# A list scheduler and its task clock charge a single-pass matmul a longer fixed time

## Chip, cores and metric

The kernel runs on one core of a Trainium2 chip. The metric is the device time of one execution in microseconds (us). A core has a tensor engine (PE, whose weight loads are shown as PEld), a vector engine (DVE), a scalar engine (ACT), GpSimd (POOL) and a sync engine (SP) that here issues DMAs only. Each executes its own instructions in the order in which the program gives them and waits for the others by semaphores.

## The reference, cut to what matters

Two layers over 512 tokens of width 1024, in float32. A layer mixes tokens by three branches, adds the input, normalizes, goes through a gated feed-forward and normalizes again:

```python
z = x @ w_in[l]                      # one projection, its columns shared out to the branches
y_a = a_b * causal_dwconv(a_c * a_v, conv_a_w)
y_b = diff_attention(dq, dk, dv, lam, lam_init, subln_g)
y_c = nsa_attention(nq, kc, ..., cmp_pos, phi_w1, phi_w2)   # compressed, selected and window keys
gates = sigmoid(m_g)
merged = sum(gates[:, :, i] * (y_i @ w_branch[i]))
x = layer_norm(ALPHA * x + merged @ w_o, ln1_g, ln1_b)
h = causal_dwconv(x @ w_up, conv_w) + conv_b
a, u = split(h)
x = layer_norm(ALPHA * x + (gelu(a) * u) @ w_down, ln2_g, ln2_b)
```

dq, dk, nq and three of the six key and value parts get rotary embeddings first.

## The kernel before, in words

Nearly all time is matrix products at float32 accuracy. Each operand is split into a high and a low part (xh and xl of the activations, wh and wl of the weights), and a product is three single-pass matmuls into one bank of PSUM, high by high, high by low and low by high (`mm3`). Weights come in 290 units of 128 x 1024 words: SP loads raw, ACT copies it to wh, DVE (or POOL, for a few units around a change of phase) subtracts to wl; raw, wh and wl have three buffers each. A projection (`g_proj`) is eight mm3 of 512 columns, 24 matmuls, into one of three banks of tag mm.

The order of the work is made in two steps, before the program is issued.

`Sched` runs tasks, which are generators that emit instructions. A task gives back a delay in ns, an event, or nothing, and the first ready task in order of priority goes on. What "ready" means is told by `sch.now`, a clock that `mm` and `tr` push on by what they think a matmul or a transpose takes on PE. The delays are the constants `DLY` (line 115): for instance `norm`, 4025 ns, from the instructions of a token tile's norm to its transposes. `g_fill` at priority 9 fills the waits with projections, gates and branches.

`Recorder.schedule` then takes all recorded instructions, with their costs by `Recorder.cost`, and lists them: on each engine, at each moment of its model, the first instruction in order of tracing whose inputs are there and whose buffers can be had goes next. `issue` emits the result in that order. So the costs decide the order on every engine; how long things take on the chip is another matter.

The pieces that the text below speaks of:

- `rope` (two operations of DVE from the bank, one of POOL, one sum on DVE) makes a query or key head ready. `g_cmp` then multiplies it with the compressed keys, four small matmuls sc<-kcc per head for four heads in a layer, after a delay `rope`.
- `g_tok_norm` makes the products with the tokens on partitions (w_o and w_dn). For each token tile of 128 the last three units are multiplied together, 3 units x 2 x 3 = 18 matmuls of 512 columns, then a task `g_norm` is started: statistics, mean, the power of the variance on POOL (`rsqrt`, out s<-s,mhalf), scaling and bias on DVE, and after `DLY["norm"]` two times four transposes (tp<-cst,tmp), each followed by a split into xh (ACT) and xl (DVE).
- `g_halves` is the next phase's beginning: three banks, first for tokens 0 to 255 and then for 256 to 511, in matmuls of 256 columns, as soon as the events of the norm allow. The weights wl of these units are made on POOL.

Of the kernel before, what the change touches and what calls it, by code (L numbers as in the profile page):

```python
# [26 lines left out]

# [1 line left out]
def _t_block(w, cols):  # L29
# [68 lines left out]
def _smalls(inp, l):  # L98
    """Per-layer constants that sit on partitions: [128, .]"""
    p = []  # L100
    p.append(inp["ffn_conv_w"][l].reshape(3, 44, 128).transpose(2, 1, 0).reshape(128, 132))
    p.append(inp["ffn_conv_b"][l].reshape(44, 128).T)
    p.append(inp["conv_a_w"][l].reshape(3, 4, 128).transpose(2, 1, 0).reshape(128, 12))
    p.append(inp["nsa_cmp_pos"][l].reshape(2, 16, 128).transpose(2, 0, 1).reshape(128, 32))
    p.append(inp["diff_subln"][l].reshape(128, 1))
    p.append(np.broadcast_to(inp["diff_lambda"][l].reshape(1, 256), (128, 256)))
    p.append(np.concatenate([inp["nsa_phi_w2"][l, i] for i in (0, 0, 1, 1)], axis=1))
    return np.concatenate(p, axis=1)
# [4 lines left out]
N_UNITS = 290  # L113
# time (ns) that the other engines take until the tensor engine can go on with what a step has made
DLY = dict(norm=4025, xsplit=2550, t2=11900, gelu=439.8, ctr=1000, rope=3680, stack=3150, cmp=40500, score=245, soft=1600, psplit=1700, pvfree=529.2, dsoft=875, dsoft_n=21, dat=200, dnorm=9000, dscore=1960)
# [4 lines left out]

# [1 line left out]
def _dims(side, sizes, known):  # L122
# [14 lines left out]
def _rearrange(idx, pattern, known):  # L137
    """einops on the free dimensions (the partition dimension p stays first)"""
    lhs, rhs = (_dims(x, None, None) for x in pattern.split("->"))
# [20 lines left out]
class RAP:  # L160
    """an access pattern of a recorded tile: where it lies, and how to get it from the real tile"""

# [44 lines left out]
class Recorder:  # L207
    # ns from the end of an instruction to the start of one that needs it
    LAT = {("PE", "PE"): 0, ("ACT", "ACT"): 0, ("DVE", "DVE"): 127, ("POOL", "POOL"): 97, ("ACT", "PE"): 230,
# [58 lines left out]
    def cost(eng, name, args, kw, op):  # L268
# [7 lines left out]
        if eng == "PE":  # L276
# [4 lines left out]
            if b.dtype == F32R:  # L281
                return nb / 2.4 + 3 if nb >= 256 else max(110, nb / 0.6)
            return 216 * max(1, nb / 128)
# [19 lines left out]
    def schedule(self):  # L303
        """list scheduling in order of tracing; slots of a tag are given in order of first use"""
        import heapq
# [26 lines left out]
        def slots(op):  # L332
            """None if the slots can be had now, else when (or inf)"""
            need = {}
# [103 lines left out]
class Sched:  # L438
    """Orders the tensor engine's work: tasks are generators that emit instructions and yield a delay in ns,
    an Event, or None; the first ready task in order of priority goes on.  now is the tensor engine's clock."""  # L440

# [31 lines left out]
def trunk(ctx, tc, xT_d, x_d, w_d, cst_d, sm_d, w1_d, gb_d, out_d, order):  # L473
# [46 lines left out]

# [1 line left out]
    def mm(o, a, b, start, stop):  # L522
        T.matmul(o, a, b, start=start, stop=stop)
        n = math.prod(b.shape[1:])
        if b.dtype == F32R:
            sch.now += n / 2.4 + 3 if n >= 256 else max(107, n / 0.6)
        else:
# [10 lines left out]

# [1 line left out]
    cst = cp.tile([128, NCST], F32, tag="cst", name="cst")  # L540
# [8 lines left out]

# [1 line left out]
    def unit(*key, parts=1, lo=None):  # L551
# [27 lines left out]
    def g_halves(x, evs, keys):  # L579
        """the first products of a phase, by token halves, as the norm before it delivers them"""  # L580
        us = []
# [26 lines left out]
    def stack_q(z, a0, a1):  # L608
        """a0 = [hi of rows 0:64; their lo], a1 = [lo of rows 64:128; their hi]"""
        lo = tmp(F32R)  # L610
# [6 lines left out]
    def stack_k(z, h0, h1, l0, l1):  # L617
        """h0 = [hi; hi] of rows 0:64, h1 of rows 64:128, l0, l1 the same of the lo parts"""
        for h, lo, r, o in ((h0, l0, LO, HI), (h1, l1, HI, LO)):
# [5 lines left out]
    def softmax(o, n, mx, sums):  # L625
        """exp((o + causal mask) / 8 - its row maximum), the row sums into sums; mx is left at minus the maximum"""
        e = tmp()
# [5 lines left out]
    def rsqrt(v, n, r=None, o=None):  # L633
        """(v + eps) ** -0.5"""
        if r is None:
# [8 lines left out]

# [1 line left out]
    def g_tok_norm(l, kind, nk, lhs, res_d, gi, last):  # L646
        """norm(ALPHA * x + lhs^T w): the next x (transposed and split, per token tile an event, and in DRAM)"""
        r, st = [], []
# [51 lines left out]
        for n in range(2):  # L700
            o = [bank(b) for b in (("mm", "mm", "mm", "sc") if n == 0 else ("sc", "pv", "mm", "mm"))]

            # the columns of a token tile's products; the very last ones in two halves, each in a bank
            cols = [[(o[t], 0, 512)] for t in range(4)]
# [39 lines left out]
    def g_layers():  # L744
# [1 line left out]
        X = new_x()  # L746
# [25 lines left out]
    def g_layer(l, X, evs, res_d):  # L772
        lam_init = 0.8 - 0.6 * math.exp(-0.3 * l)

# [1 line left out]
        smf = cp.tile([128, 176], F32, tag="smf", name=nm("smf"))  # L776
# [10 lines left out]

# [1 line left out]
        ya, yb, yc = [None, None], [None, None], [None, None]  # L789
# [55 lines left out]

# [1 line left out]
        okc, ovc, oks = yield from g_halves(X, evs, [(l, "n_kv", 0), (l, "n_kv", 1), (l, "n_kv", 2)])  # L847
# [10 lines left out]
        def g_compress(i, z):  # L858
# [7 lines left out]
            for a in range(2):  # L866
                Y.dma_start(w1[a], w1_d[l, i, :, a * 1024:(a + 1) * 1024])
            # rows of the product: hi and lo of the windows; columns: with hi and with lo of the weights
            o = bank("sc")
# [57 lines left out]

# [1 line left out]
        onv = [bank(b) for b in ("mm", "mm", "mm", "pv")]  # L929
        for k0, k1 in ((0, 3), (3, 6), (6, 8)):  # L930
            w = unit(l, "n_v", (k0, k1))
            for t in range(4):
# [3 lines left out]
                yield None  # L936
        # per token tile and branch [hi of group 0, its lo, lo of group 1, its hi], 64 columns each
        gate = cp.tile([128, 4, 24], F32, tag="gate", name=nm("gate"))
# [52 lines left out]

# [1 line left out]
        yc[0], yc[1] = big(F32R), big(F32R)  # L993
# [33 lines left out]
        def g_nsa_out():  # L1027
# [3 lines left out]
            for u, (qt, g, b) in enumerate(units):  # L1031
# [27 lines left out]
                if b == 0:  # L1059
                    continue  # L1060
                # rows of this group: products with hi of V; the other rows: with lo of V
                if g == 0:
# [17 lines left out]

# [1 line left out]
        ev_d = [Event() for _ in range(4)]  # L1082
# [111 lines left out]

# [1 line left out]
        mh = [big(F32R), big(F32R)]  # L1196
# [5 lines left out]

# [1 line left out]
        hb = []  # L1204
# [63 lines left out]
```

## Time and profile before

| | |
|---|---|
| median of 3 runs | 1825.97 us (1824.64 to 1826.08) |
| profiled execution, span from its first to its last instruction | 1823.5 us |
| PE busy | 1796.3 us (99%) |
| DVE busy | 1108.0 us (61%) |
| ACT busy | 777.7 us (43%) |
| POOL busy | 216.8 us (12%) |
| mean granted clock of PE | 0.998 of 2.4 GHz |

The page of the profile gives the profiled execution by its span; the times of the runs hold what lies around it as well. Spans of matmuls in the timeline overlap, since the next one starts before the last is through; what one costs in a stream is read from start to start.

### The profile page before, as it was taken

To read this page: it belongs to the slowest core of one execution; us is meant where nothing else is said; L and a number is where in the kernel's file an instruction comes from. 1 tells how busy PE (TensorE), PEld (TensorE's weight loads), DVE (VectorE), ACT (ScalarE), POOL (GpSimd) and SP (SyncE) were. 2 spreads that over 40 slices of the span, in tenths; PEclk is the share of its full clock that TensorE was granted. 3 is DMA by queue.
4 is the path that set the end of the run, shared out by engine and by line. 5 is a ranking of instruction groups with operands and counts; after the bars stand their busy time and mean duration, and the time that the engine had idled before them with its cause. 6 is when DMAs were issued, how large, how long until landed. Compare 5 with 4: busy or idle time off the path is not lost.

```text
span 1823.5 us, 23236 instructions
## 1 busy us (share of the span) xinstructions
PE 1796.3 (99%) x8794; PEld 1506.6 (83%) x8794; DVE 1108.0 (61%) x1987; ACT 777.7 (43%) x1340; POOL 216.8 (12%) x264
## 2 busy tenths in 40 slices
PE   8999999999999999999999999999999999999997
PEld 7788888888888888888887888888888888888886
DVE  6968968534457566643389688674344666566334
ACT  4548854422324444421244587553223244444211
POOL 1300123000021000000234001120000400000004
PEclk9999999999999999999999999999999999999999
DMA  6520243233234223423254203332333333234221
GB/s 220 153 90 24 60 133 95 91 104 126 96 105 153 100 92 104 139 95 103 93 166 132 76 25 96 101 104 83 108 133 97 123 127 99 98 104 138 94 93 70
DMA packets 60976, 193.36 MB, mean 106 GB/s; under 512 B 7680, under 2 KB 9824, under 8 KB 60736
## 3 DMA queue, kind: packets, MB, share of 16 engines
q1 hardware_dynamic: 49984, 167.01, 27.6%
q0 software_dynamic: 10880, 24.88, 5.4%
q8 instruction: 69, 1.13, 0.3%
q14 instruction: 43, 0.35, 0.1%
HBM read 171.93 MB, written 8.39 MB: 99 GB/s over the span
## 4 chain that ended last, share of the span: by engine, by line
PE 90%; DVE 6%; issue 1%; ACT 1%; POOL 1%; DMA 1%; SPq 0%; POOLq 0%; DVEq 0%; ACTq 0%
PE mm L421 72%; PE sc L421 8%; PE pv L421 6%; DVE tmp L421 4%; PE tp L421 3%; DVE wl L421 1%; DVE s L421 1%; POOL tmp L421 1%; ACT tmp L421 0%; DMA tmp<-in_xT_dram 0%; DVE xl L421 0%; POOL s L421 0%; DVE big L421 0%; ACT big L421 0%; DMA big<-big 0%
## 5 line engine op out<-in xcount | busy, mean ns | idle before, releaser
L421 PE MATMUL mm<-xh,wh 128*128 128x512 f32 (+1 forms) x1632 | 619.9, 381 | 9.0 <-ACT wh L421 5.2
L421 PE MATMUL mm<-xl,wh 128*128 128x512 f32 (+1 forms) x1632 | 619.9, 380 | 3.0 <-DVE xl L421 2.5
L421 PE MATMUL mm<-xh,wl 128*128 128x512 f32 (+1 forms) x1632 | 619.6, 380 | 0.2
L421 DVE TENSOR_TENSOR wl<-raw,wh 128x1024 fp32r<-128x1024 f32 (+2 forms) x270 | 331.8, 1230 | 437.7 <-ACT wh L421 433.6
L421 ACT ACTIVATE wh<-raw 128x1024 fp32r<-128x1024 f32 (+2 forms) x291 | 306.1, 1052 | 523.5 <-PE mm L421 336.4
L421 PEld LDWEIGHTS mm<-xh,wh 128*128 128x128 f32 x1632 | 308.0, 189 | 62.3 <-ACT wh L421 5.2
L421 PEld LDWEIGHTS mm<-xl,wh 128*128 128x128 f32 x1632 | 308.7, 189 | 57.1 <-DVE xl L421 4.5
L421 PEld LDWEIGHTS mm<-xh,wl 128*128 128x128 f32 x1632 | 308.3, 189 | 56.3 <-DVE wl L421 1.3
L421 PE MATMUL mm<-wh,big 128*128 128x512 f32 (+1 forms) x600 | 187.9, 382 | 0.0
L421 ACT ACTIVATE tmp<-tmp,s 128x512 f32<-128x512 f32 (+3 forms) x261 | 140.5, 558 | 63.5 <-DVE s L421 47.0
L421 DVE SCALAR_TENSOR_TENSOR tmp<-mm,smf,tmp 128x511 f32<-128x511 f32 (+1 forms) x176 | 131.3, 746 | 3.1
L421 PEld LDWEIGHTS mm<-wh,big 128*128 128x128 f32 x600 | 111.8, 188 | 21.9
L421 ACT ACTIVATE big<-tmp 128x512 fp32r<-128x512 f32 (+1 forms) x100 | 62.9, 629 | 142.9 <-DVE tmp L421 142.2
L421 PE MATMUL mm<-big,wh 128*128 128x512 f32 x384 | 120.2, 392 | 0.0
L421 PE MATMUL mm<-wl,big 128*128 128x512 f32 (+1 forms) x300 | 114.4, 381 | 0.0
L421 DVE CUSTOM_DVE_ANT_0 tmp<-sc,cst 128x512 f32<-128x512 f32 (+3 forms) x192 | 90.0, 482 | 25.2 <-PE sc L421 24.0
L421 POOL TENSOR_TENSOR wl<-raw,wh 128x1024 fp32r<-128x1024 f32 x21 | 51.5, 2463 | 369.0 <-ACT wh L421 369.0
L421 POOL TENSOR_TENSOR tmp<-tmp,cst 128x512 f32<-128x512 f32 (+1 forms) x46 | 52.0, 1137 | 320.8 <-ACT pt L421 123.6
L421 ACT ACTIVATE tmp<-tmp 128x512 f32<-128x512 f32 (+2 forms) x68 | 41.2, 606 | 113.0 <-DVE tmp L421 112.7
L421 PE MATMUL tp<-cst,tmp 128*128 128x128 f32 x544 | 85.3, 272 | 0.2 <-ACT tmp L421 0.2
L421 PEld LDWEIGHTS mm<-big,wh 128*128 128x128 f32 x384 | 71.6, 188 | 14.6
L421 PE MATMUL sc<-wh,big 128*128 128x512 f32 x240 | 80.5, 390 | 0.0
(145 smaller groups left out, 2070.6 us busy)
## 6 DMA issues: line engine op xcount, KB each, us to landing
raw<-in_w_dram SPq DMA_DIRECT2D x283, 512.0 KB, 3.3
big<-big POOLq DMA_DIRECT2D x48, 128.0 KB, 2.8
res<-tmp SPq DMA_DIRECT2D x24, 256.0 KB, 2.0
tmp<-res POOLq DMA_DIRECT2D x24, 256.0 KB, 3.1
w<-in_w_dram SPq DMA_DIRECT2D x8, 512.0 KB, 5.1
pt<-in_gb_dram POOLq DMA_DIRECT2D x16, 256.0 KB, 4.3
tmp<-tmp POOLq DMA_DIRECT2D x20, 128.0 KB, 2.3
tmp<-in_xT_dram SPq DMA_DIRECT2D x8, 256.0 KB, 7.1
```

What stands on the lines that cost most here:

```text
L421: op.call(*[f(x) for x in op.args], **{k: f(v) for k, v in op.kw.items()})
```

## The change

In both places where a matmul of 256 columns or more with a float32r operand is costed, the fixed part of 3 ns becomes 13.6 ns. For 512 columns that is 226.9 ns in place of 216.3, for 256 columns 120.3 in place of 109.7.

```diff
@@ Recorder.cost
             if b.dtype == F32R:
-                return nb / 2.4 + 3 if nb >= 256 else max(110, nb / 0.6)
+                return nb / 2.4 + 13.6 if nb >= 256 else max(110, nb / 0.6)
             return 216 * max(1, nb / 128)
@@ mm, in trunk
         if b.dtype == F32R:
-            sch.now += n / 2.4 + 3 if n >= 256 else max(107, n / 0.6)
+            sch.now += n / 2.4 + 13.6 if n >= 256 else max(107, n / 0.6)
         else:
             sch.now += 214 * max(1, n / 128)
```

No instruction is added or removed; the order on the engines changes, and with it the buffers that tiles get. Other lines of the diff are comments.

**The compressed scores on PE, first layer.** tmp is the roped query head, mm_622 (mm_636 after the change) the bank that it came from, and the next projection's 24 matmuls go to mm_688 (mm_692). Before:

```order
L421 MATMUL mm_688<-xl_102,wh_614 128x512
L421 MATMUL mm_688<-xh_98,wl_634 128x512
L421 MATMUL mm_688<-xh_98,wh_614 128x512
L421 MATMUL sc_730<-kcc_624,tmp_695 128x64 x4
L421 MATMUL mm_688<-xl_102,wh_614 128x512
L421 MATMUL mm_688<-xh_98,wl_634 128x512
L421 MATMUL mm_745<-xh_98,wh_660 128x512
```

After:

```order
L421 MATMUL mm_692<-xh_98,wl_627 128x512
L421 MATMUL mm_733<-xh_98,wh_654 128x512
L421 MATMUL mm_733<-xl_102,wh_654 128x512
L421 MATMUL sc_736<-kcc_617,tmp_703 128x64 x4
L421 MATMUL mm_733<-xh_98,wl_668 128x512
```

The scores of the first head stood two matmuls before the end of the next projection, and now stand two matmuls into the one after it. The other three heads move by 6, 8 and 13 matmuls, and the second layer has the same numbers.

**The transposes on PE where w_o of the first layer ends and w_up begins.** mm_4777 and mm_4784 are the banks of the third and the fourth token tile, mm_4938 (mm_4947) the first of the next phase. Before:

```order
L421 MATMUL mm_4777<-wh_4794,big_4461 128x512
L421 MATMUL tp_4881<-cst,tmp_4592 128x128 x4
L421 MATMUL mm_4784<-wh_4743,big_4242 128x512
...
L421 MATMUL mm_4784<-wh_4794,big_4461 128x512
L421 MATMUL tp_4928<-cst,tmp_4601 128x128 x4
L421 MATMUL mm_4938<-xh_4887,wh_4897 128x256
L421 MATMUL tp_4940<-cst,tmp_4622 128x128 x4
L421 MATMUL mm_4938<-xl_4915,wh_4897 128x256
```

After:

```order
L421 MATMUL mm_4777<-wh_4743,big_4247 128x512
L421 MATMUL tp_4857<-cst,tmp_4592 128x128 x4
L421 MATMUL mm_4777<-wh_4757,big_4456 128x512
...
L421 MATMUL mm_4777<-wh_4794,big_4461 128x512
L421 MATMUL tp_4890<-cst,tmp_4600 128x128 x4
L421 MATMUL mm_4784<-wh_4743,big_4242 128x512
...
L421 MATMUL mm_4784<-wh_4794,big_4461 128x512
L421 MATMUL tp_4939<-cst,tmp_4620 128x128 x4
L421 MATMUL mm_4947<-xh_4865,wh_4909 128x256
```

The first token tile's transposes (tmp_4592 and tmp_4601, now tmp_4600) lay on both sides of the fourth tile's products and now both stand ahead of them; of the second tile's (tmp_4613 and tmp_4622, now tmp_4620) the last keeps its place.

**POOL at the same place.** wl are the low parts of the next phase's first weights, s the variance with eps, s<-s,mhalf its power; s_4974 (s_4949) is the third token tile's. Before:

```order
L421 TENSOR_TENSOR wl_4912<-raw_4775,wh_4897 128x1024
L421 TENSOR_TENSOR wl_4942<-raw_4790,wh_4919 128x1024
L421 TENSOR_SCALAR s_4974<-s_4934 128x1
L421 TENSOR_TENSOR wl_4978<-raw_4815,wh_4931 128x1024
L421 TENSOR_TENSOR s_5004<-s_4974,mhalf 128x1
```

After:

```order
L421 TENSOR_TENSOR wl_4921<-raw_4774,wh_4909 128x1024
L421 TENSOR_SCALAR s_4949<-s_4934 128x1
L421 TENSOR_TENSOR wl_4952<-raw_4788,wh_4927 128x1024
L421 TENSOR_TENSOR s_4979<-s_4949,mhalf 128x1
L421 TENSOR_TENSOR wl_4989<-raw_4814,wh_4943 128x1024
```

The power of the third tile's variance stood behind three wl and now stands behind two.

## Rows read from the trace of the kernel before

**Rows 1.** The page: span, busy time of the engines, granted clock by slices.
```profile
span 1823.5 us, 23236 instructions
...
PE 1796.3 (99%) x8794; PEld 1506.6 (83%) x8794; DVE 1108.0 (61%) x1987; ACT 777.7 (43%) x1340; POOL 216.8 (12%) x264
...
PEclk9999999999999999999999999999999999999999
```

**Rows 2.** Stretches: from:to, length, us (instructions) of PE, PEld, DVE, ACT, POOL, PEclk, DMA.
```profile
50.00:100.00 50.00, 48.34 (x236) 39.10 (x235) 46.63 (x99) 26.24 (x46) 19.02 (x25) 1.00 0.45 131
100.00:200.00 100.00, 100.00 (x528) 83.68 (x527) 78.85 (x195) 71.19 (x160) 0.60 (x1) 1.00 0.17 54
200.00:300.00 100.00, 99.37 (x507) 82.48 (x506) 76.33 (x205) 57.41 (x137) 22.20 (x32) 1.00 0.35 98
505.00:562.00 57.00, 56.05 (x311) 48.54 (x311) 32.02 (x50) 13.87 (x17) 22.16 (x18) 1.00 0.41 136
562.00:900.00 338.00, 338.00 (x1511) 280.68 (x1510) 172.60 (x203) 124.06 (x152) 12.00 (x12) 1.00 0.32 105
900.00:950.00 50.00, 48.39 (x343) 45.26 (x342) 43.82 (x80) 21.51 (x41) 19.67 (x21) 1.00 0.48 148
950.00:1000.00 50.00, 48.21 (x235) 38.84 (x234) 46.54 (x95) 26.44 (x46) 18.85 (x25) 1.00 0.49 139
1100.00:1220.00 120.00, 119.13 (x611) 98.64 (x610) 94.59 (x248) 70.16 (x169) 28.24 (x40) 1.00 0.35 100
1405.00:1465.00 60.00, 59.05 (x326) 51.10 (x325) 33.80 (x53) 14.65 (x18) 22.16 (x18) 1.00 0.40 137
```

**Rows 3.** The list of waits of PE: total us, times, longest.
```profile
PE mm L421 <- DVE xl L421: 2.5, 3, 0.8
PE sc L421 <- DVE s L421: 1.4, 4, 0.5
PE sc L421 <- DVE tmp L421: 1.0, 2, 0.5
```

**Rows 4.** One stretch, instructions on tile mm alone (columns: no POOL).
```profile
349.00:505.00 156.00, 155.77 (x687) 128.60 (x686) 13.06 (x19) 10.99 (x19) 1.00 0.33 109
```

**Rows 5.** Timeline of PE at the first and last compressed scores: start, us, shapes, [idle before].
```profile
64.62 0.39 PE L421 MATMUL mm<-xh,wh 128*128 128x512 f32 x1
65.51 1.08 PE L421 MATMUL sc<-kcc,tmp 128*128 128x64 f32 x8 [0.49 <-DVE tmp L421]
...
86.47 0.39 PE L421 MATMUL mm<-xl,wh 128*128 128x512 f32 x1
87.06 0.96 PE L421 MATMUL sc<-kcc,tmp 128*128 128x64 f32 x7 [0.21 <-DVE s L421]
```

**Rows 6.** Busy time from 58 to 92 us.
```profile
58.00:92.00 34.00, 32.72 (x156) 26.13 (x156) 32.79 (x64) 14.78 (x21) 17.35 (x23) 1.00 0.49 138
```

**Rows 7.** Timeline of PE at the first change of phase.
```profile
549.30 0.28 PE L421 MATMUL mm<-xh,wh 128*128 128x256 f32 x1
550.42 0.39 PE L421 MATMUL mm<-xl,wh 128*128 128x256 f32 x1 [0.84 <-DVE xl L421]
```

**Rows 8.** Timeline of POOL at the first change of phase.
```profile
543.19 4.77 POOL L421 TENSOR_TENSOR wl<-raw,wh 128x1024 fp32r<-128x1024 f32 x2 [2.44 <-ACT wh L421]
548.55 2.85 POOL L421 TENSOR_TENSOR wl<-raw,wh 128x1024 fp32r<-128x1024 f32 x1
551.36 1.01 POOL L421 TENSOR_TENSOR s<-s,mhalf 128x1 f32<-128x1 f32 x1
```

**Rows 9.** Timeline of DVE at the first change of phase.
```profile
546.54 2.63 DVE L421 SCALAR_TENSOR_TENSOR tmp<-tmp,s,pt 128x512 f32<-128x512 f32 x2
549.09 1.27 DVE L421 TENSOR_TENSOR xl<-tp,xh 128x512 fp32r<-128x512 f32 x2
552.41 2.74 DVE L421 SCALAR_TENSOR_TENSOR tmp<-tmp,s,pt 128x512 f32<-128x512 f32 x4 [0.46 <-POOL s L421]
```

**Rows 10.** Timeline of DVE at the end of the program.
```profile
1815.29 0.74 DVE L421 SCALAR_TENSOR_TENSOR tmp<-tmp,s,pt 128x512 f32<-128x512 f32 x1
```

## Prediction, made before the changed kernel was run

> **What bounds the kernel now.** I read the page first, then the work of each stretch, the list of waits, and last the rows of the places that wait. The page shows TensorE (PE) busy for 99% of the span, with the granted clock at its upper level, 2.4 GHz, in every slice [rows 1], 1.00 in each stretch shown [rows 2]. The stretches come next: in the long feed-forward one, PE is busy for all of its 338 us, and the places with idle time are few [rows 2], the start and the tail left aside. They are the end of each layer's projections with the start of its attention (50 to 100 and 950 to 1000 us, 1.7 and 1.8 us idle), the change from a product over token tiles to the next phase (505 to 562, 900 to 950 and 1405 to 1465 us, 0.95, 1.61 and 0.95 us), and the attentions (0.63 and 0.87 us). No instruction is added or removed by this change, so the work of PE stays; all that can change is some of this idle time, which comes to about 8.5 us in all, or idle time that does not exist yet. The list of waits says who is late: VectorE (DVE) with xl at the phase changes, and with tmp or s where the scores with the compressed keys (sc<-kcc) wait for their query [rows 3].
>
> **Is the new charge right?** In the gate stretch, 687 matmuls of 512 columns fill 155.77 us [rows 4]: 226.7 ns each. The planner charged 216.3 ns before and charges 226.9 ns now. So its clock ran 4.6% fast against PE and now agrees with it. That it now agrees is no time by itself: what follows is where its order then differs.
>
> **First part: the compressed scores, eight places.** In the order of before, the four sc<-kcc matmuls of a query head stand 22, 23, 24 and 26 projection matmuls after the end of that query's bank (heads 0 to 3, the same in both layers); in the changed order 26, 29, 32 and 39. The query has to go through four rope operations, one of them on POOL, before it can be used. The rows show PE waiting there every time: start to start, the step onto the first head's scores takes 0.89 us, of which a matmul is 0.23, so 0.66 us is lost; on the last head's 0.59 - 0.23 = 0.36 us [rows 5]. Eight such places at the mean of these two come to 4.1 us; the list of waits counts 1.4 + 1.0 = 2.4 us of idle time for six of them [rows 3], from modelled ends, so lower. The new lead is longer by 4, 6, 8 and 13 matmuls, that is 0.91, 1.36, 1.81 and 2.95 us, more than any one wait. It must also make up for the waits before it that go away, since the query then is no earlier while PE is: the last head loses at most three waits of 0.66 us ahead of it, 1.98, and its own 0.36, and has 2.95. So the waits should vanish, if DVE is not slower there. But DVE is the engine that is full: 32.79 of 34 us [rows 6]. PE will run ahead of a DVE that cannot follow, and part of the time may come back as a wait after 92 us. I take 2.9 us saved, about seven tenths of 4.1; bounds 0 and 4.1.
>
> **Second part: three changes of phase.** A norm task waits 4025 ns on the planner's clock before its transposes may be written. A token tile is 18 matmuls: 18 x 216.3 = 3894 ns before, so the transposes came two tiles later; 18 x 226.9 = 4085 ns now, so they come one tile later. In the order, three of the four transposes around the last token tile move ahead by half a tile or more, and those of the third token tile (tmp_4632, now tmp_4631) come 30 matmuls of 256 columns into the new phase, where there were 53. But what they transpose is made by DVE and POOL, whose work has not become shorter.
>
> Before, PE ran 28 matmuls of the new phase and then waited for xl from 549.30 to 550.42, of which a matmul is 0.12: 1.0 us lost [rows 7]. DVE was late since it had two operations with two inputs in SBUF beside POOL's wl, 2.63 us for two, then the two xl from 549.09, 1.27 us [rows 9]. Now one of these two xl comes before them, so the one that PE needs is ready 0 to 0.6 us earlier than at 550.3: 549.7 to 550.3. PE asks for it after 17 matmuls, 11 of 0.12 us earlier in its order, so at 548.1 in place of 549.4. The first wait grows from 1.0 to between 1.6 and 2.2 us, less what the two xl sharing the place gained: say 1.0 to 2.0. Then the transposes of the third tile follow 13 matmuls or 1.6 us later, at 550.7 to 551.7. They need POOL's power of the variance and a scaling on DVE. POOL's power stood behind three wl, at 551.36 [rows 8]; now behind two: 543.19 + 4.77 for two, some 0.6 for the small addition that took POOL to 548.55, and 1.01, so done at 549.6. DVE then does statistics and two scalings of 0.69 us each, or 1.3 beside POOL (four took 2.74 alone, two took 2.63 beside it [rows 9]): ready at 551.2 to 552.3, a second wait of 0 to 0.9 us in all. Against 1.0 us before, and a later wait of 0.27 us that I leave as it is, the loss is between nothing and 1.9 us for one change of phase; the middle, and a little more since DVE has its operations beside POOL for most of this time, is 1.2 us. Three times that is **3.6 us**, bounds -1 (all of the earlier start pays) and +6.
>
> Does DVE wait for POOL, or only run slower beside it? Rows 9 show each operation stretched from 0.69 to 1.3 us, while the wl beside them took 2.4 us. The Trainium skill, SBUF — State Buffer, section "Who interferes with whom", says that a VectorE instruction with two SBUF inputs and a GpSimd instruction that reads SBUF exclude each other: the later one blocks until the other has ended. By that section the operations ahead of the xl would end only after the second wl, by my estimate 1.2 us later per phase change, and the sum would be 3.6 us more. The trace does not agree: an operation that had waited out a wl would take up to 3 us, and the two take 2.63 us together [rows 9].
>
> **Small parts.** At the very end, a scaling on DVE (0.74 us [rows 10]) now stands ahead of the last residual addition, from which the chain to the last store starts: +0.5 us, bounds 0 and 0.7. In the attentions the leads are dealt out anew. The idle there is 0.63 and 0.87 us [rows 2], and some leads (transposes that wait for DVE) get shorter by some 5% as counted in matmuls, which is what the truer clock takes away; others grow. I take +0.8 us for both layers, bounds -1.5 (all of it goes) and +3 (it triples). In the long feed-forward stretch [rows 2] the order is the same: nothing.
>
> **Sum.** -2.9 + 3.6 + 0.5 + 0.8 = +2.0 us. The profiled execution's span is 1823.5 us [rows 1], so 1825.5; the median of the runs, 1825.97, lies 2.5 us above that span. The forecast is **1828.0 us**. About 0.2% (3.65 us) is what a measurement of this kernel can tell from no change, so this counts as the same.
>
> **Rivals.** *Slower: DVE's queue at the phase changes sets the time.* The transposes are written earlier but DVE and POOL take as long, and DVE executes in order, so each xl pushed forward delays the scalings behind it. Price 2.5 us a phase change, 7.5 us: -2.9 + 7.5 + 1.3 = +5.9, 1831.9 us. It decides from (3.65 + 2.9 - 1.3) / 3 = 1.75 us a change on. For it: DVE's queue already makes PE wait at all three places [rows 3], and PE now asks 1.3 us earlier. Against it: POOL's power comes one wl sooner. Chance 0.29.
>
> *Slower: DVE and POOL exclude each other.* If an operation of DVE had to wait out a wl of POOL's (2.4 us, half of 4.77 [rows 8]) where it starts behind one, it would end up to 1.7 us later than the stretched 1.3 us; with 1.2 us for each phase change the sum is +5.6 us, 1831.6 us. For it: the stretching itself. Against it: two operations beside POOL took 2.63 us [rows 9]. Chance 0.03. This is the rule of the Trainium skill, SBUF — State Buffer, section "Who interferes with whom".
>
> *Faster: the leads pay in full.* The compressed scores give 4.1 us, nothing comes back later since DVE is busy for only 78.85 of the 100 us that follow [rows 2], and the phase changes save 0.3 us each since POOL's power and DVE's queue start earlier: -5.0, 1821.0 us. For it: each new lead exceeds its wait. Against it: DVE at 32.79 of 34 us [rows 6]. Chance 0.18.
>
> *Nothing, net.* The planner's order is new at many places, but the work of PE fills 99% of the span and waits merely move: 1826.0 us. Chance 0.10; my forecast itself has 0.40.
>
> **How the numbers follow.** The forecast and the empty case make "same": 0.50. Slower 0.29 + 0.03 = 0.32, faster 0.18. The range takes in the slower case with a little beyond, and the faster one up to its last us: 1822.0 to 1833.0; the least cases of both sides are left out with 1 in 10 each.
>
> **What would show it.** In the profile after, the waits of sc on DVE tmp and s should be nearly gone from the list, and DVE should be as full as before between 58 and 92 us. The wait of mm for DVE xl should be longer than 0.8 us at each phase change and be followed by a wait of tp for DVE tmp, which the list of before does not have. Idle time of 2 us or more near 545 to 555 us says the second part is right; under 1.3 us says it is wrong, and the time is then near 1824. If sc still waits for DVE in the attention's start, the first part is wrong, and the time is above 1830.

## The result, and the profile after

The changed kernel takes 1841.97 us (median, 1840.62 to 1842.69), the kernel before 1825.31 us beside it: a ratio of 1.0091, 95% interval 1.0077 to 1.0105. It is 16.7 us **slower**; the forecast was 1828.0, with a range to 1833.0 and a chance of 0.32 for slower. The profiled execution's span grew by 16.4 us.

The page of the changed kernel; PE has the work that it had [rows 1], spread over a longer span:

```profile
span 1839.9 us, 23262 instructions
...
PE 1802.1 (98%) x8794; PEld 1509.9 (82%) x8794; DVE 1110.7 (60%) x1987; ACT 775.6 (42%) x1340; POOL 219.0 (12%) x264
```

The stretches after the change, with the columns of [rows 2]; the phase changes lie later in the program than before, so the last stretch is longer:

```profile
50.00:100.00 50.00, 48.54 (x234) 39.79 (x235) 44.84 (x96) 25.02 (x44) 17.91 (x25) 1.00 0.44 128
...
200.00:300.00 100.00, 97.96 (x492) 80.43 (x491) 74.05 (x194) 55.57 (x133) 22.64 (x32) 1.00 0.34 98
505.00:562.00 57.00, 54.18 (x275) 46.07 (x274) 32.46 (x51) 12.47 (x16) 21.99 (x18) 0.97 0.38 126
...
900.00:950.00 50.00, 47.18 (x313) 43.56 (x312) 38.35 (x64) 14.52 (x20) 21.89 (x22) 0.97 0.35 112
...
1100.00:1220.00 120.00, 117.93 (x600) 97.50 (x601) 93.21 (x244) 69.10 (x165) 24.33 (x33) 1.00 0.31 91
1405.00:1480.00 75.00, 71.19 (x364) 60.56 (x363) 40.99 (x59) 17.45 (x23) 21.79 (x18) 0.98 0.35 119
```

Two things meet the eye. The phase changes lose 2.8 to 3.8 us of PE's time, where it was 0.95 to 1.61, and there the granted clock is below 1.00 in the mean, which it was in none of [rows 2]. And the late attentions lose 2.0 us each, where it was 0.63 and 0.87.

The list of waits of PE after the change names the first; it stands at the top, and the list of before [rows 3] does not have it:

```profile
PE tp L421 <- DVE tmp L421: 11.0, 8, 2.7
...
PE pv L421 <- ACT tmp L421: 2.7, 2, 1.3
...
PE sc L421 <- DVE tmp L421: 0.8, 2, 0.4
PE sc L421 <- DVE s L421: 0.6, 2, 0.3
```

To see where the 16.7 us are, I summed PE's time from start to start over all matmuls and took off what each shape takes in a stream (226.5 ns for 512 columns, 120 for 256, 108.5 for 128 and so on). What is left is waiting, or a slower clock, by place of the program, in us; both layers are put together. E1 to E18 are the experiments below.

| | start of layers | compressed scores | attention, first part | attention, late part | three phase changes |
|---|---|---|---|---|---|
| before | 8.9 | 7.6 | 6.9 | 5.7 | 5.4 |
| after | 10.0 | 5.5 | 7.4 | 10.7 | 17.2 |
| E1 | 10.5 | 6.7 | 8.3 | 10.4 | 9.9 |
| E2 | 8.3 | 5.3 | 6.7 | 8.0 | 6.8 |
| E7 | 10.0 | 3.6 | 8.0 | 6.3 | 5.0 |
| E13 | 9.8 | 3.7 | 7.3 | 3.8 | 17.0 |
| E17 | 9.8 | 6.0 | 7.6 | 10.6 | 6.1 |
| E18 | 9.5 | 4.0 | 7.1 | 3.8 | 6.1 |
| E16 | 8.0 | 3.6 | 7.4 | 3.9 | 5.0 |

So the phase changes cost 11.8 us more, the late part of the attentions 5.0, the starts 1.1, and the compressed scores give 2.1 back.

**One phase change, after.** PE's timeline: the third token tile's transposes start 3.00 us after the matmul ahead of them, 2.9 us of it lost, and from 556.4 on the matmuls of 256 columns start 0.21 us apart, for another 3 us, where 0.12 is the rule.

```profile
552.04 0.28 PE L421 MATMUL mm<-xh,wh 128*128 128x256 f32 x1
555.04 0.63 PE L421 MATMUL tp<-cst,tmp 128*128 128x128 f32 x4 [2.72 <-DVE tmp L421]
...
556.81 0.42 PE L421 MATMUL mm<-xl,wh 128*128 128x256 f32 x1
557.02 0.41 PE L421 MATMUL mm<-xh,wl 128*128 128x256 f32 x1
```

The two stretches of it; the granted clock is 1.00 while PE stands and 0.53 behind it, that is mostly the lower level of 1.2 GHz:

```profile
552.00:555.00 3.00, 0.32 (x3) 0.12 (x1) 2.92 (x2) 0.00 (x0) 2.98 (x3) 1.00 0.53 175
...
556.40:560.00 3.60, 3.60 (x20) 3.60 (x19) 3.21 (x6) 0.58 (x1) 2.57 (x5) 0.53 1.00 304
```

What PE waits for, on POOL and on DVE. The whole phase lies 2.46 us later in this trace: POOL's first wl starts at 545.65, where [rows 8] had it at 543.19. POOL's power of the variance is done at 552.05, where [rows 8] had it at 552.37; against the start of the phase it comes 2.8 us sooner, about the length of the wl that it was moved past. Then POOL starts its third wl, and DVE its first scaling, at nearly the same time:

```profile
545.65 2.40 POOL L421 TENSOR_TENSOR wl<-raw,wh 128x1024 fp32r<-128x1024 f32 x1 [2.72 <-ACT wh L421]
...
551.47 0.58 POOL L421 TENSOR_TENSOR s<-s,mhalf 128x1 f32<-128x1 f32 x1
552.00 2.35 POOL L421 TENSOR_TENSOR wl<-raw,wh 128x1024 fp32r<-128x1024 f32 x1
```

```profile
552.08 2.82 DVE L421 SCALAR_TENSOR_TENSOR tmp<-tmp,s,pt 128x512 f32<-128x512 f32 x1 [0.77 <-POOL s L421]
```

```profile
554.82 0.74 DVE L421 SCALAR_TENSOR_TENSOR tmp<-tmp,s,pt 128x512 f32<-128x512 f32 x1
```

The first scaling takes 2.82 us, the second, with no wl beside it, 0.74: the first waits out the wl. The kernel before shows the same with the subtraction of the mean, if one asks for single operations instead of the pair of [rows 9]:

```profile
546.54 1.97 DVE L421 SCALAR_TENSOR_TENSOR tmp<-tmp,s,pt 128x512 f32<-128x512 f32 x1
```

2.63 us for two was 1.97 and 0.74 with some overlap at the ends, not twice 1.3; the second wl had started at 545.6 and ended at 548.0 [rows 8].

**One place of the late attention**, in the first layer. After the change DVE's wl comes at 258.57, beside POOL's part of the rope, and takes 1.90 us; the score reductions are queued behind it. Before, it came behind them, alone, and took 1.22. After:

```profile
258.57 1.90 DVE L421 TENSOR_TENSOR wl<-raw,wh 128x1024 fp32r<-128x1024 f32 x1
```

```profile
258.09 1.29 POOL L421 TENSOR_TENSOR tmp<-tmp,cst 128x512 f32<-128x512 f32 x1
```

```profile
263.74 0.71 PE L421 MATMUL pv<-big,tmp 128*128 128x128 f32 x4 [1.33 <-ACT tmp L421]
```

Before, on DVE and on PE:

```profile
260.65 1.22 DVE L421 TENSOR_TENSOR wl<-raw,wh 128x1024 fp32r<-128x1024 f32 x1
```

```profile
262.72 0.49 PE L421 MATMUL pv<-big,tmp 128*128 128x128 f32 x2 [0.50 <-ACT tmp L421]
```

### The profile page after: what moved, and what is told of

Same layout as the page of the kernel before. It is cut to its first block, busy times and chain, and to the rows that moved or that the text cites. A ratio compares the mean times of both kernels' runs of the same rounds, so it can differ in the third digit from the quotient of the medians.

```text
span 1839.9 us, 23262 instructions
## 1 busy us (share of the span) xinstructions
PE 1802.1 (98%) x8794; PEld 1509.9 (82%) x8794; DVE 1110.7 (60%) x1987; ACT 775.6 (42%) x1340; POOL 219.0 (12%) x264
## 4 chain that ended last, share of the span: by engine, by line
PE 87%; DVE 6%; issue 3%; POOL 2%; ACT 1%; DMA 1%; SPq 0%; DVEq 0%; ACTq 0%; POOLq 0%
PE mm L421 70%; PE sc L421 8%; PE pv L421 6%; DVE tmp L421 4%; PE tp L421 3%; DVE wl L421 1%; POOL s L421 1%; POOL tmp L421 1%; ACT tmp L421 1%; DVE s L421 0%; ACT wh L421 0%; DMA big<-big 0%; DMA w<-in_w_dram 0%; DMA tmp<-in_xT_dram 0%; POOL wl L421 0%
## 5 line engine op out<-in xcount | busy, mean ns | idle before, releaser
L421 DVE TENSOR_TENSOR wl<-raw,wh 128x1024 fp32r<-128x1024 f32 (+2 forms) x270 | 335.8, 1244 | 454.7 <-ACT wh L421 451.7
L421 PEld LDWEIGHTS tp<-cst,tmp 128*128 128x128 f32 x544 | 67.0, 141 | 27.5 <-issue 12.4
```

The lines of the kernel that those rows point to most:

```text
L421: op.call(*[f(x) for x in op.args], **{k: f(v) for k, v in op.kw.items()})
```

## The experiments

Two theories at first. **L**: the list scheduler's dearer PE makes all other engines look early, and it takes away leads that had, unknown to it, covered DVE and POOL blocking each other. **N**: the norm delay, which used to end two token tiles later and now ends one later, is what costs. All times are medians; a ratio is to the kernel before in the same runs. The diffs are cut to the lines that matter, and the comments in them are added here.

**E1, only the list scheduler's cost raised.**

```diff
@@ mm (against the changed kernel)
-            sch.now += n / 2.4 + 13.6 if n >= 256 else max(107, n / 0.6)
+            sch.now += n / 2.4 + 3 if n >= 256 else max(107, n / 0.6)
```

> Only the list scheduler's cost is raised; the task clock keeps 3 ns. Theory L (the list scheduler, with PE costed longer, puts the third token tile's transposes and POOL's power of its variance one wl earlier, and DVE's scaling then meets POOL's wl): the long wait of tp for DVE tmp at the three phase changes stays, 2.5 to 3 us each, and the time is 1835 to 1842 us. Theory N (the norm delay, which now ends before the second token tile instead of after it, is what costs): the waits go, the time is 1824 to 1831 us.

1836.36 us, 1.0058 (1.0041 to 1.0075). The waits stay, though at 1.7 us and not at 2.5 to 3:

```profile
PE tp L421 <- DVE tmp L421: 5.5, 5, 1.7
...
PE mm L421 <- POOL wl L421: 3.1, 3, 1.0
```

Two thirds of the loss come from this one line. The clock does not fall here.

**E2, only the task clock raised** (the other line undone).

> Only the task clock is raised; the list scheduler keeps 3 ns. Theory L: no wait of tp above 1.5 us at the phase changes, no fall of the granted clock there, 1821 to 1830 us; the compressed scores keep their longer leads (32, 31, 41 and 42 matmuls or so), so their waits are nearly gone. Theory N: the long waits stay, 1835 to 1842 us.

1825.1 us, 0.9999 (0.9990 to 1.0008). As L says. The phase changes cost 6.8 us, and no wait of tp is in the list; the compressed scores still wait for DVE s, 1.0 us, which is not "nearly gone". Alone, the task clock is free; it is not free on top of E1.

**E3, norm delay 4100.**

```diff
-DLY = dict(norm=4025, xsplit=2550, ...
+DLY = dict(norm=4100, xsplit=2550, ...
```

> The change as it is, with the norm delay at 4100 ns, above 18 x 226.9 = 4085. Theory N: the phase changes go back to the waits of before, some 11 us are given back, 1829 to 1833 us. Theory L: POOL's and the third tile's order is that of the change, the waits stay within 0.5 us of it, 1838 to 1843 us.

1834.51 us, 1.0051 (1.0036 to 1.0066): 7.5 us given back, between the two. The crossing of the tile boundary is a cause, but only with the dearer PE in the list scheduler: in E2 it is crossed as well. At 9.9 us the phase changes are where E1 has them, with POOL's order of the change in both.

**E4, POOL's third wl behind both powers.** The planner gets a dependence that the data do not have.

```diff
@@ g_halves
+                    if late:                       # the third unit of a phase
+                        rec.lo.deps[rec.pow.i] = rec.pow
```

> The change as it is, but at the phase changes the planner holds POOL's third wl back behind the power of the fourth token tile's variance, so that DVE's two scalings of the third tile (3.48 us for two after the change) have no wl beside them. Theory L with exclusion of DVE and POOL: the two scalings take 1.4 us, the wait for the third tile's transposes falls from 2.9 to 0.7 to 1.2 us, the granted clock stays at 1.00, and with 3 to 3.5 us less per phase change the time is 1831 to 1834 us. If DVE and POOL only slow each other down a little, as the prediction took it: the wait falls by at most 1 us each, 1838 to 1841 us.

1839.03 us, 1.0073 (1.0058 to 1.0088). The two scalings of the third tile do take 1.42 us, and the wait for its transposes falls to 0.64 us. But the next operation of DVE then meets the wl, and the fourth tile waits instead:

```profile
552.35 1.42 DVE L421 SCALAR_TENSOR_TENSOR tmp<-tmp,s,pt 128x512 f32<-128x512 f32 x2 [0.77 <-POOL s L421]
...
553.86 2.71 DVE L421 SCALAR_TENSOR_TENSOR tmp<-tmp,s,pt 128x512 f32<-128x512 f32 x1
```

```profile
553.25 0.63 PE L421 MATMUL tp<-cst,tmp 128*128 128x128 f32 x4 [0.64 <-DVE tmp L421]
...
558.64 0.63 PE L421 MATMUL tp<-cst,tmp 128*128 128x128 f32 x4 [1.94 <-DVE tmp L421]
```

The exclusion is shown; the repair only moved it by one tile.

**E5, the exclusion by itself**, in a program of DVE's and POOL's operations alone.

> A program of its own that computes none of the reference: it runs DVE's operation with two inputs in SBUF (512 columns) alone, POOL's subtraction of 1024 columns alone, and then side by side, first with two SBUF inputs on DVE, then with one of them in PSUM, then with DVE's statistics (one input), and last DVE's two-input operation beside POOL's power of a single column. If DVE and POOL exclude each other where both read SBUF for two inputs: beside the subtraction, single operations of DVE take 2.5 to 3.2 us and the rest 0.7, and with a PSUM input or a single input all take 0.7. If they only slow each other down: all of them take 1.2 to 1.4 us.

On DVE, two operations with both inputs in SBUF beside POOL's wl, then one with an input in PSUM beside it:

```profile
44.53 5.57 DVE L421 SCALAR_TENSOR_TENSOR tmp<-tmp,sone,pt 128x512 f32<-128x512 f32 x2
```

```profile
33.22 0.74 DVE L421 SCALAR_TENSOR_TENSOR tmp<-tmp,sone,mm 128x512 f32<-128x512 f32 x1
```

POOL beside the first, and beside the second:

```profile
44.01 2.79 POOL L421 TENSOR_TENSOR wl<-raw,wh 128x1024 fp32r<-128x1024 f32 x1
```

```profile
31.92 2.35 POOL L421 TENSOR_TENSOR wl<-raw,wh 128x1024 fp32r<-128x1024 f32 x1
```

Each of the two takes 2.8 us, a whole wl and its own time; with an input in PSUM nothing is blocked on either side. The Trainium skill, SBUF — State Buffer, section "Who interferes with whom", says that a VectorE instruction with two SBUF inputs contends with a GpSimd instruction that reads SBUF, and that the one that comes second blocks until the other is through; the trace agrees. The statistics, with one input, kept their 0.67 us beside the wl. The last pair of the plan, DVE's operation beside POOL's power, shows nothing: the power ran when DVE's operations were over. And one input is not always free, for a copy of 8 columns on DVE lasted as long as the wl beside it, where other such copies took 0.16 us:

```profile
27.02 2.30 DVE L421 COPY hand<-hand 128x8 f32<-128x8 f32 x1 [5.93 <-POOL hand L421]
```

**E6, PE kept busy in the wait**, with 24 matmuls that nobody reads.

```diff
@@ g_norm, third tile, ahead of its transposes
+                for c in range(24):
+                    d = T.matmul(idle[:, 0:128], swap, swap, start=True, stop=True)
+                    d.cost, d.deps[scaled.i] = 0, scaled
```

> The change as it is, with 24 matmuls of 128 columns that nobody reads, 2.6 us of added work, put on PE directly ahead of the third tile's transposes at the three phase changes, where it waits for 2.9 us. If the fall of the granted clock behind the wait costs what the rows show (some 20 matmuls of 256 columns at 0.21 in place of 0.12 us): the clock stays at 1.00 there and 1.5 to 2.2 us are given back at each, 1835.5 to 1838 us. If it is the wait alone that costs: 1841 to 1843 us.

1840.01 us, 1.0079 (1.0063 to 1.0094): 2.0 us less than the change, with work added. Behind the wait the clock stays at 1.00:

```profile
552.00:555.50 3.50, 3.50 (x34) 3.50 (x32) 2.73 (x2) 0.00 (x0) 3.50 (x4) 1.00 0.47 150
555.50:560.00 4.50, 4.39 (x39) 4.28 (x38) 4.46 (x9) 1.19 (x2) 2.22 (x4) 1.00 0.76 228
```

Start to start, the added matmuls counted as loss, the first two phase changes lose 1.5 us less each. At the third the fourth tile then waits for 2.48 us in place of 0.89, which eats it up. So the price of the fall is 1.5 us each, as the rows at 0.21 us said.

**E7, every other cost, latency and delay of the planner times 1.049.**

```diff
+F = 1.049
+DLY = {k: v * F for k, v in DLY.items()}
...
+            op.cost *= F          # all but single-pass matmuls of 256 columns or more
```

> The change, with every other cost, latency and delay of the planner multiplied by 1.049, the ratio of 226.9 to 216.3. Theory R (the planner's other costs were as short of the chip's as PE's was, so that raising PE's alone made the others look early): the order comes near that of before and the time goes back to 1823 to 1829 us. If a longer PE cost is harmful by itself: 1835 us or more.

1822.94 us, 0.9987 (0.9978 to 0.9996). With PE at its measured cost and the rest stretched in the same ratio, the loss is gone. So it is not the number for PE that costs, but the ratio. That is nearly so by construction: a list made with all costs in the old ratio is nearly the old list (only the matmuls of 256 columns, 120.3 ns in place of 109.7, are stretched by more than 1.049). E7 does not tell which of the other costs was too short.

**E8, the kernel before with more lead for the compressed scores.**

```diff
@@ g_cmp
+            yield 2000
             yield ev_kcc
```

> The kernel before, with 2000 ns more delay ahead of the compressed scores, nothing else: leads of 33, 30, 30 and 27 matmuls in place of 22, 23, 24 and 26. If the gain that the prediction took for the longer leads is there by itself: 2.9 us less than before (up to 4.1), and no wait of sc for DVE tmp or s. If DVE, nearly full there, gives it back later: within 1 us of before.

1828.96 us, 1.0018 (1.0009 to 1.0027): 3.4 us slower. The scores' own waits shrink by about 1.7 us in the sums, less than the 2.9 asked for, and those for DVE s stay in the list with 1.1 us; at the end of the selected attention, where the kernel before had none, PE now waits, in both layers:

```profile
222.57 0.51 PE L421 MATMUL pv<-pt,big 128*128 128x512 f32 x1 [0.34 <-ACT pt L421]
223.41 0.33 PE L421 MATMUL tp<-cst,tmp 128*128 128x128 f32 x1 [0.34 <-ACT tmp L421]
...
224.46 0.55 PE L421 MATMUL tp<-cst,tmp 128*128 128x128 f32 x3 [0.44 <-DVE tmp L421]
```

A longer lead at one place is paid for at another, some 140 us later.

**E9, E10: the exclusion put into the planner**, on the changed kernel (E9) and on E7 (E10).

```diff
@@ schedule
+                    if op.lock:   # DVE with two SBUF inputs, or POOL on more than 8 columns
+                        op.start = max(t, held["POOL" if e == "DVE" else "DVE"])
+                        held[e] = op.start + op.cost
```

> The change, and the planner also lets a DVE operation with two SBUF inputs and a POOL operation on more than 8 columns wait for each other, as the program of e5 showed them to. If the exclusion, left out of the planner, is all that the short PE cost had covered: the long waits at the phase changes and the longer ones in the attentions go, 1822 to 1830 us. If the planner only knows of the exclusion but has no slack left for it: the order at the phase changes stays that of the change (POOL's third wl still right behind the power) and the time is 1834 to 1843 us.

> The planner of e7 (every other cost times 1.049), with the exclusion of e9 in it. If knowing of the exclusion helps where the slack is there: 1817 to 1822 us. If e7's slack already covers it: 1821 to 1826 us.

1836.34 us, 1.0058 (1.0044 to 1.0071), and 1831.1 us, 1.0030 (1.0018 to 1.0041). By the sums of waits both repair the late attentions (4.0 us in each, of 10.7 and 6.3) and both make the phase changes dearer than in the kernel before (20.2 and 16.2 us). In E9 the list still starts the third wl as soon as it may, and the third tile's two scalings meet it (3.51 us for two). In E10 POOL's order is that of before, and yet the loss is there: DVE stands until the power comes, with the second tile's xl queued behind the scalings, and PE waits for the third wl (1.84 us) and for the xl (1.01 us).

```profile
547.90 1.42 DVE L432 SCALAR_TENSOR_TENSOR tmp<-tmp,s,pt 128x512 f32<-128x512 f32 x2 [2.77 <-POOL s L432]
```

So POOL's order alone does not set the price of a phase change.

**E11, E12: E7 with other factors**, 1.025 and 1.08.

> The planner of e7 with a factor of 1.025 in place of 1.049. POOL's order at the phase changes is again that of the change (power of the third tile behind two wl). Theory R, with a step where that order turns: 1829 to 1836 us, nearer to the list scheduler's change alone (1836.4) than to e7 (1822.9). If the time follows the factor smoothly: 1830 us would be half way between 1842 and 1823, 1832 us.

> The planner of e7 with a factor of 1.08. If more slack than the ratio of before still helps: 1815 to 1822 us. If the leads are long enough at 1.049 and longer ones only cost buffers: 1822 to 1830 us.

1828.68 us, 1.0019 (1.0010 to 1.0028), and 1825.94 us, 1.0005 (0.9996 to 1.0014). Over the factor the time goes 1842.0, 1828.7, 1822.9, 1825.9: no step at 1.025 and lower than both readings that I gave, with POOL's order still that of the change. Too much lead costs again, mostly in the first part of the attentions (12.5 us in place of 8.0).

**E13, the exclusion in the planner, but not for POOL's wl**, so that only the rope's operation counts on POOL.

```diff
-(eng == "POOL" and len(wide) > 0)
+(eng == "POOL" and len(wide) > 0 and args[0].tile.tag != "wl")
```

> The change, with the exclusion of DVE and POOL in the planner as in e9, but not for POOL's wl, so that the phase changes keep the order of the change. If the longer waits in the late part of the attentions (5.4 and 5.3 us after the change, 3.1 and 2.5 before) come from DVE blocked behind POOL's part of the rope, unknown to the planner: they fall to 2.2 and 1.9 us, the phase changes keep their 17 us, and the time is 1833 to 1837 us. If e9's gain there came from something else, the wl's: 1839 to 1843 us.

1832.98 us, 1.0043 (1.0030 to 1.0057). 9.0 us less than the change: the late attentions fall from 10.7 to 3.8 us, below before, the compressed scores from 5.5 to 3.7, and the phase changes keep their 17.

**E14, the third tile's transposes 23 matmuls further back on PE; E15, with E13.**

```diff
@@ g_norm, and where the list makes users ready
+                    if t == 2:
+                        scaled.late = 2700
...
-                        u.ready = max(u.ready, op.end + lat)
+                        u.ready = max(u.ready, op.end + lat + op.late)
```

> The change, with the planner told that the third token tile's scalings are of use 2700 ns later, so that PE's queue has its transposes 23 matmuls of 256 columns further back; POOL's order stays that of the change. If the loss at the phase changes is the place of these transposes in PE's order, ahead of a scaling that waits out POOL's wl: the wait of 2.9 us and the fall of the clock behind it go, 3.5 to 4.5 us at each, 1828 to 1832 us. If PE then only waits for the same scalings elsewhere: 1838 us or more.

> e13 and e14 together. If the two are separate causes and between them the whole of the loss: their gains add, 1820 to 1825 us.

1842.59 us, 1.0098 (1.0084 to 1.0112), and 1831.59 us, 1.0034 (1.0022 to 1.0046). No gain for E14, and for E15 1.4 us over E13, within the scatter of the runs: the third tile no longer waits, but the fourth does, for the chain on DVE is as late as it was.

```profile
562.88 1.12 PE L422 MATMUL tp<-cst,tmp 128*128 128x128 f32 x4 [2.30 <-DVE xl L422]
```

So the place of the transposes on PE is not the cause by itself; what they wait for, the chain of POOL and DVE, is late wherever they stand.

**E17, POOL's order of before inside the changed kernel**, and **E18, with E13's exclusion**.

```diff
@@ g_halves
+                    if late:                       # the third unit: the third tile's power waits for it
+                        rec.pows[-2].deps[rec.lo.i] = rec.lo
```

> The change, with POOL's order at the phase changes as before: the power of the third tile's variance behind the third wl, so that DVE's four scalings run with no wl beside them; the planner then puts the third tile's transposes 53 matmuls into the new phase of its own accord. If the order on POOL is what the loss at the phase changes hangs on: waits of 1.5 to 2.7 us at each in place of 5.2 to 6.7, the granted clock at 1.00, 1829 to 1833 us. If the earlier transposes of the first two tiles cost by themselves: 1836 us or more.

> e17 with the exclusion of e13 in the planner, PE at its measured cost and no other cost touched. If POOL's order at the phase changes and the unknown exclusion beside the rope are separate and between them the whole loss: 1820 to 1825 us, as fast as before or faster. If they overlap: above 1826 us.

1831.28 us, 1.0032 (1.0020 to 1.0044), and **1821.65 us**, 0.9979 (0.9971 to 0.9988). With all three wl first, the power starts at 554.26, over 2 us later, and the four operations of DVE behind it (the third tile's two scalings, then one subtraction of the mean and one scaling of the fourth) run with no wl beside them, 2.74 us for the four:

```profile
549.08 5.22 POOL L421 TENSOR_TENSOR wl<-raw,wh 128x1024 fp32r<-128x1024 f32 x2
554.26 1.01 POOL L421 TENSOR_TENSOR s<-s,mhalf 128x1 f32<-128x1 f32 x1
```

```profile
551.96 2.89 DVE L421 SCALAR_TENSOR_TENSOR tmp<-tmp,s,pt 128x512 f32<-128x512 f32 x1
555.31 2.74 DVE L421 SCALAR_TENSOR_TENSOR tmp<-tmp,s,pt 128x512 f32<-128x512 f32 x4 [0.46 <-POOL s L421]
```

What waits out the third wl now is a subtraction of the fourth tile's mean (2.89 us), and it is through before the power. The phase changes fall from 17.2 to 6.1 us. The two repairs add: -10.7 (E17) and -9.0 (E13) make -19.7, and E18 is 20.3 us below the change.

**E16, E7 with E13's exclusion.**

> e7, with e13's exclusion in the planner. If e10 lost its 8 us by the wl's at the phase changes alone (5.0 to 6.2 us of waits each, 1.7 in e7) and had gained 2 us in the attentions: 1819 to 1822 us, below both kernels. If not: above 1823 us.

**1819.13 us**, 0.9971 (0.9961 to 0.9982): 6 us below before and 23 below the change, the fastest of the study. Of the waits that this text is about, its list has only the one at the phase changes left, as it was before [rows 3]:

```profile
PE mm L432 <- DVE xl L432: 2.5, 3, 0.8
```

## Why the prediction was wrong

**The new charge**: right. PE is costed as the trace shows it, and that alone is worth nothing (E2) or harm (E1). The prediction said that the agreement is no time by itself, but not why the old one did good: the planner did not know of the exclusion, and with a PE that ran 4.6% fast in its model it put more of PE's work between a result's start and its use than it would have with the true one. That this was the cover fits E7, E13, E17 and E18 at the phase changes and in the late attention.

**Compressed scores**: -2.9 forecast, -2.1 by the sum of waits. The mechanism held, and so did the doubt about DVE: E8 shows that a longer lead alone comes back as waits at the end of the attention. But the waits of sc for DVE were to be nearly gone from the list, and they fell from 2.4 to 1.4 us.

**Phase changes**: +3.6 forecast, +11.8 measured; this is the step that failed. Of its two waits, the first (mm for xl, 1.0 to 2.0 us forecast) turned out smaller: from 549.65 to 550.74 PE starts four matmuls and loses 0.6 us, and the list after has no wait of mm for DVE xl. The second (the third tile's transposes, "0 to 0.9 us in all") is 2.9 us. The step failed in three terms.
- "Only runs slower beside it" was read from two operations shown in one row of [rows 9]. Single operations take 1.97 and 0.74 us: exclusion, not stretching. The price of a scaling, "0.69 us each, or 1.3 beside POOL", was 2.82 us where it started with the wl (the rows after the change; E5 shows the same price by itself). The prediction's "The trace does not agree" rests on this misreading. The rival that had the mechanism was given 0.03, and its 1.2 us a phase change was too small as well: the scaling alone lost 2.1 us, and the clock's price came on top.
- That "POOL's power comes one wl sooner" was counted as a gain. It did come sooner, by the whole wl: the forecast end of 549.6 is 552.06 in a phase that lies 2.46 us later, and 552.05 was measured. But that put the scaling beside the third wl, and the fourth tile's power came only at 557.37, behind that wl and a wait of POOL for DVE. E17 puts POOL's order back, the planner then puts the third tile's transposes back to 53 matmuls as well, and 10.7 us return; the transposes' place alone gave nothing (E14). POOL's order of before with the transposes left at 30 was not tried.
- The granted clock was not in the sum. Behind the wait of 2.9 us it falls for some 3 us, at 1.5 us a time (E6, first two phase changes); before, no wait at a phase change was longer than 1.0 us, and it fell at none.

The cause was also named wrongly in part: the norm delay against 18 matmuls explains why the first two tiles' transposes move, and with the dearer list cost it is worth 7.5 us (E3), but POOL's order turns with the list scheduler's line alone (E1, not E2). Both are needed for the full loss: with POOL's order of the change and no crossing the phase changes cost 9.9 us (E1, E3), with the crossing and POOL's order of before 6.8 and 6.1 (E2, E17), with both 17.2.

**Small parts**: +0.8 forecast for the attentions, +5.0 in their late part and +0.5 in their first. I had no row of a single place there. E13 shows the cause: once the planner knows of the exclusion beside the rope, the late part is at 3.8 us. **The tail**: +0.5 forecast; from PE's last start to the end of the span it is 1839.9 - 1829.74 = 10.2 us, 10.4 before, so nothing.

The sum's sign was right, its size was not, and the median lies 9 us above the range. Of the tests that the prediction set, idle time of 2 us or more at the phase changes and the wait of tp for DVE tmp came true, but the first said no more than that some wait is there: it could not tell the forecast's mechanism from the rival's. The longer wait of mm for DVE xl did not come. Two of its readings were loose without weight: a 9 in the slices stands for 90% or more of the clock, and in the second layer the lead of head 0 goes to 25 matmuls, not 26. DVE between 58 and 92 us is less full than forecast:

```profile
58.00:92.00 34.00, 33.19 (x160) 26.93 (x158) 30.77 (x60) 14.40 (x20) 15.13 (x21) 1.00 0.45 132
```

Not settled: why the start of the layers costs 1.1 us more was not tried, and that E16 beats E18 by 2.5 us is by place mostly the start of the layers and the phase changes, with no test of which line does it.

## What to carry to other kernels

In a planner, one cost made true can make the whole worse when others stay untrue: what counts is the ratio of the engines' costs, and a cheap PE may be the slack that covers what the model leaves out. Find the unmodelled thing first and correct it together with the cost: E18 beats the kernel before, its two halves E13 and E17 alone do not. More truth in the model is not enough either: the whole exclusion (E9, E10) did worse than the part that leaves out the wl (E13, E16). And ask the trace for single operations before believing a mean: a pair at 2.63 us was one blocked and one free.

## What the runs showed of the hardware

- A DVE operation with two inputs in SBUF and a POOL operation block each other for a whole operation: 2.82 us in place of 0.74, POOL's wl 2.79 in place of 2.35 (E5). Whoever is late pays: a scaling that could start 2.8 us sooner met a wl and took 2.1 us longer.
- In E5 a POOL operation on 8 columns took as long as a train of eleven such DVE operations beside it; it ended only when the train was over (the page counts spans on POOL as rough):

```profile
12.59 7.29 POOL L421 TENSOR_SCALAR hand<-hand 128x8 f32<-128x8 f32 x1
```

- A DVE copy of 8 columns with a single input lasted 2.30 us beside a wl, to the wl's end (E5), so the blocking was not limited to two inputs.
- At the three phase changes of the change the granted clock fell to its lower level 1.4, 1.1 and 0.05 us after PE had started again behind a wait of 2.7 us in the list, and stayed there for about 3 us; matmuls of 256 columns then started 0.21 us apart. The length of the wait alone does not tell whether it falls: behind 1.7 us (E1), 1.9 us (E4, first two phase changes) and 2.5 us (E6, third) it did not, behind 1.9 us at E4's third it did (0.61 in the mean over the next 4 us), and in E12 it did behind waits of 1.30 and 0.45 us in the second layer (0.50 from 1127.95 to 1131.35 us), where the same two waits in the first layer left it at 1.00.
